# Value products in groups of four key blocks, with the recurrence's tiled products behind them, in a hybrid attention and RWKV-7 encoder block

## Chip, cores and metric

The kernel runs on one core of one Trainium2 chip. The metric is the device time of one execution in microseconds (us). Three runs of the kernel before gave 3750.1, 3751.88 and 3755.33 us; the median is 3751.88 us.

## What is computed

One encoder block over 2048 tokens of width 1024. Two head groups read one input projection: eight heads of softmax attention over two key and value heads, and eight heads of a recurrence (RWKV-7) that runs over the tokens in both directions. Their outputs are joined and projected. Then 16 expert networks each take the 256 tokens that suit them best. The change touches the middle only, where attention and recurrence run beside each other ("the mixers"):

```python
def one_block(qi):                                   # 128 queries
    s = jnp.einsum('bqhgd,bkhd->bhgqk', qi, k) * scale
    p = jax.nn.softmax(s, axis=-1)
    return jnp.einsum('bhgqk,bkhd->bqhgd', p, v)

def step(S, inp):                                    # S: 64 x 64 per head
    r_t, w_t, k_t, v_t, kk_t, a_t = inp
    sa = jnp.einsum('bhvk,bhk->bhv', S, -kk_t)
    S = (S * w_t[:, :, None, :] + sa[..., None] * (kk_t * a_t)[:, :, None, :]
         + v_t[..., None] * k_t[:, :, None, :])
    return S, jnp.einsum('bhvk,bhk->bhv', S, r_t)
```

## The kernel before

The program has four stages: input projection, mixers, output projection, experts. Attention in the mixers goes through 16 blocks, each of two heads and 512 queries (`attention`, `att_out`). One round of `att_out` takes one of 16 key blocks `kb` of 128 keys: scores for both heads into the PSUM tile `st_ps` (lines 694 and 695, two matmuls for each head, since numbers are kept as a high and a low part), one exponential on ScalarE into `pt` (line 696), additions into `acc` for the softmax's sum on VectorE and GpSimd (699), and after every second round the value products of two key blocks into `o_ps` (line 686). A value product has 64 output rows a head, so the two heads take the left and the right half of the array's 128 columns: the profile writes this 128*64, rows times columns of the slice that a matmul uses. `st_ps` has one buffer of two banks, `pt` three.

Beside that, `att_max` finds each query's largest score for the next block (`s_ps`, lines 647 and 648, reduced on VectorE in line 649). The 8 columns of maxima are turned into rows by 8 matmuls with an identity (line 660, 128*2), and ScalarE copies them into rows 64 and 65 of `qa` (662), where the scores' second matmul subtracts them.

The recurrence (`rwkv`) takes 16 sequences of 16 chunks of 64 tokens, four chunks at a time: 64 quarters. `rw_a1` loads `xin`, makes the chunk products of one head after the other (line 846, 64 rows of the array, so 64*128), masks them into `r56` on VectorE (849), transposes `xin` (854) and stores a part for the triangular solve (`rw_solve`, on VectorE or GpSimd). `rq_av` multiplies by 64*64 slices (line 961), `rq_wu` (971), `rq_l` (983) and `rq_step` (999) take the whole array; `rq_step` is the chain from chunk to chunk.

`mixers` calls the two generators in turn, one round of each, four rounds of the recurrence to a quarter, so a quarter lies beside four key blocks. A list scheduler then sets each engine's order: by the order of the calls, unless a block stands under `high_priority`, and by when its own model takes an instruction to be ready. On the chip each engine runs its list in that order. `issue_after(x)`, which the change uses, puts an instruction behind `x` on x's engine.

Of the kernel before, what the change touches and what calls it, by code (L numbers as in the profile page):

```python
# [583 lines left out]
PTB = 3  # L584
# [5 lines left out]
class Attention(Encoder):  # L590
    def attention_pools(self, c):
# [9 lines left out]
        self.kl1 = self.a_k.tile([66, T], F32R, name="kl1")  # L601

# [19 lines left out]
    def att_max(self, j, qc, keys, res):  # L622
# [30 lines left out]
        hl = self.a_q.tile([P, 8, 2], F32R, tag="mhl", name="mhl")  # L653
        nc.vector.tensor_copy(out=hl[:, :, 0], in_=nm)
        nc.vector.tensor_tensor(out=hl[:, :, 1], in0=nm, in1=hl[:, :, 0].bitcast(F32), op=ALU.subtract)
# [19 lines left out]
    def att_out(self, keys, v, q):  # L675
# [7 lines left out]
        def values(kb):  # L683
            pt = pts.pop(kb)
            for h in range(2):
                nc.tensor.matmul(av[64 * h : 64 * h + 64, :], v[:, kb, :], pt[:, h, :], start=(kb == 0), stop=(kb == 15), tile_position=(0, 64 * h))  # L686
# [23 lines left out]
        values(14)  # L710
        values(15)
# [54 lines left out]
class Rwkv(Attention):  # L766
    def rwkv_pools(self, c):
# [4 lines left out]
        slots = {"c": pool("rw_r0", 1)}  # L772
        self.r_m, self.r_x = pool("rw_m"), pool("rw_x", 2)
        slots["a"], slots["b"] = pool("rw_r1", 4), pool("rw_r2", 4)

        of = {(0, 0): "c", (0, 1): "a", (0, 2): "a", (0, 3): "a", (1, 0): "a", (1, 1): "b", (1, 2): "b", (1, 3): "b", (2, 0): "b"}
        for n in range(2, 16):
            for q in range(4):
                if (n, q) not in of:
                    of[n, q] = of[n - 2, q - 1] if q else of[n - 3, 3]  # L780
        self.r56_of = lambda n, q: slots[of[n, q]]
        self.gn_of = slots["b"]
# [43 lines left out]
    def rw_a1(self, n, g):  # L826

        nc = self.nc
        ct, d, half = g["id"]
        c0 = half * GC  # L830
        g["r56"] = {}
        banks = cycle(("pa", "pb", "pc") if n == 1 else ("pa",))
        mask = self.masks[d]
        for i0, q in enumerate(range(4) if d == 0 else range(3, -1, -1)):
            X = self.r_x.tile([P, 2, 512], F32, tag="xin", name="xin")
            r0 = c0 // 2 + 2 * q
            nc.sync.dma_start(out=X, in_=self.d_x[d, ct, :, r0 : r0 + 2, :])
            r56 = self.r56_of(n, i0).tile([P, 4, 384], F32, tag="r56", name="r56")
            g["r56"][q] = r56
            rv = r56.rearrange("p c (x k) -> p c x k", k=64)  # L840
            for h in range(2):
                hs = slice(64 * h, 64 * h + 64)
                p1 = self.bank(next(banks)).tile([P, 4, P], F32, tag="p", name="p1")
                for i in range(4):
                    xr, u = X[hs, i // 2, :], i % 2
                    nc.tensor.matmul(p1[:, i, :].rearrange("p (x k) -> p x k", k=64), xr[:, 128 * u : 128 * u + 128],
                                     xr[:, 256:512].rearrange("p (x u k) -> p x u k", x=2, u=2)[:, :, u, :], start=True, stop=True)
                dst = rv[:, :, 0:3:2, :] if h == 0 else rv[:, :, 3:5, :]
                nc.vector.tensor_tensor(out=dst, in0=p1.rearrange("p c (x k) -> p c x k", k=64),
                                        in1=mask.unsqueeze(1).to_broadcast([P, 4, 2, 64]), op=ALU.mult)  # L850
                yield
            p2 = self.bank(next(banks)).tile([P, 4, P], F32, tag="p", name="p2")
            for i in range(4):
                nc.tensor.transpose(p2[:, i, :], X[:, i // 2, 128 * (i % 2) : 128 * (i % 2) + 128], self.ident)
            nc.scalar.copy(out=rv[:, :, 1:6:4, :], in_=p2.rearrange("p c (x k) -> p c x k", k=64))
            for h in range(2):
                nc.sync.dma_start(out=self.d_a[n, 16 * h + 4 * q : 16 * h + 4 * q + 4].rearrange("c s t -> s c t"), in_=r56[0:64, :, 192 * h : 192 * h + 64])
            yield
# [129 lines left out]
    def rq_step(self, Q, i):  # L988
# [9 lines left out]
        for h in range(2):  # L998
            nc.tensor.matmul(p6[:, c, h, :], lc[:, c, h, :], s0[:, h, :], start=True, stop=True)
# [67 lines left out]
    def rwkv(self):  # L1067
# [23 lines left out]
        for i, (n, k) in enumerate(quarters):  # L1091
# [19 lines left out]
            def extra():  # L1111
                run(a1, 1)
                if k < 3:
# [501 lines left out]
```

## Time and profile before

| | |
|---|---|
| median of three runs | 3751.88 us |
| the profiled execution | 3751.49 us |
| its span, first to last instruction | 3749.8 us |
| TensorE busy | 3509.9 us, 94% |
| VectorE busy | 2516.7 us, 67% |
| ScalarE busy | 1755.2 us, 47% |
| GpSimd busy | 1512.5 us, 40% |
| mean granted TensorE clock | 0.957 of full speed |

Busy is the time in which an engine has at least one instruction under way. TensorE's matmuls overlap, so the time that one adds is read from start to start, not from its own duration; a float32 matmul is recorded as two passes.

### The profile page before, as it was taken

Reading aid. Unit: us, or ns where it says so; the run is one execution under the profiler, and the core shown is the slowest. Engines: PE = TensorE matmul, PEld = TensorE weight load, DVE = VectorE, ACT = ScalarE, POOL = GpSimd, SP = SyncE. Lnnn points to the kernel's source line nnn. Section 1 sums busy time; section 2 is a strip of 40 time slices with the busy share of each in tenths; the row PEclk is TensorE's granted clock in tenths of the full one; section 3 lists DMA queues with packets and bytes.
Section 4 is the critical chain, followed back from the end, with each engine's and each line's share of the span. In section 5 each row is a group of like instructions: output and inputs, shape, how many; then the busy total and the mean of one; then the engine's idle time right before and its main releaser. Section 6 shows DMA issues by size and latency. Waiting matters only on the chain. (4 is left out here: it accounts for less than half of the span.)

```text
span 3749.8 us, 61495 instructions
## 1 busy us (share of the span) xinstructions
PE 3509.9 (94%) x23436; PEld 2856.7 (76%) x23436; DVE 2516.7 (67%) x4289; ACT 1755.2 (47%) x3066; POOL 1512.5 (40%) x1484
## 2 busy tenths in 40 slices
PE   6998899799999999999999997993999999999998
PEld 5887788656666666676666664772999999999997
DVE  6688778876857778558867675447555656655653
ACT  4445444414555555545555564231444444444443
POOL 3445344526263353663364554332332332322321
PEclk8999899879999999999999998996999999999999
DMA  5335334443323433433333232443566766767664
GB/s 182 105 130 168 112 113 141 139 129 73 91 68 79 121 95 85 114 88 87 84 85 85 69 82 82 156 145 113 188 206 205 222 202 216 218 203 222 220 199 127
DMA packets 531228, 510.93 MB, mean 136 GB/s; under 512 B 213304, under 2 KB 449954, under 8 KB 525812
## 3 DMA queue, kind: packets, MB, share of 16 engines
q1 hardware_dynamic: 520612, 472.08, 41.1%
q0 software_dynamic: 10000, 34.91, 4.0%
q8 instruction: 185, 3.03, 0.3%
q14 instruction: 111, 0.91, 0.1%
q10 hardware_dynamic: 320, 0.00, 0.0%
HBM read 392.57 MB, written 109.07 MB: 134 GB/s over the span
## 5 line engine op out<-in xcount | busy, mean ns | idle before, releaser
L1452 DVE TENSOR_TENSOR w_lo<-w_raw,w_hi 128x2048 fp32r<-128x2048 f32 x189 | 432.3, 2293 | 385.8 <-ACT w_hi L1449 385.4
L1516 PE MATMUL gu<-hh,w_lo 128*128 128x256 f32 x2048 | 573.5, 280 | 0.0
L1516 PE MATMUL gu<-hl,w_hi 128*128 128x256 f32 x2048 | 572.7, 280 | 0.0
L1516 PE MATMUL gu<-hh,w_hi 128*128 128x256 f32 x2048 | 572.5, 280 | 0.0
L699 POOL TENSOR_TENSOR acc<-acc,pt 128x512 f32<-128x512 f32 x256 | 354.9, 1391 | 469.0 <-ACT pt L696 456.0
L1449 ACT CAST w_hi<-w_raw 128x2048 fp32r<-128x2048 f32 x192 | 366.9, 1912 | 319.9 <-PE down L1539 133.3
L696 ACT ACTIVATE pt<-st_ps 128x1024 f32<-128x1024 f32 x256 | 262.2, 1024 | 394.8 <-PE st_ps L695 221.2
L649 DVE TENSOR_REDUCE mx<-s_ps 128x1 f32<-128x512 f32 x512 | 342.6, 681 | 149.7 <-PE s_ps L648 148.2
L247 PE MATMUL proj_ps<-hh,w_hi 128*128 128x258 f32 (+1 forms) x1280 | 375.3, 294 | 32.8 <-DVE s_k L265 23.8
L1516 PEld LDWEIGHTS gu<-hh,w_lo 128*128 128x128 f32 x2048 | 388.0, 189 | 0.0
L1516 PEld LDWEIGHTS gu<-hh,w_hi 128*128 128x128 f32 x2048 | 385.6, 188 | 1.3
L1516 PEld LDWEIGHTS gu<-hl,w_hi 128*128 128x128 f32 x2048 | 385.5, 188 | 1.4
L247 PE MATMUL proj_ps<-hl,w_hi 128*128 128x258 f32 (+1 forms) x1280 | 373.0, 292 | 6.4 <-DVE hl L149 5.9
L247 PE MATMUL proj_ps<-hh,w_lo 128*128 128x258 f32 (+1 forms) x1280 | 371.5, 290 | 0.0
L149 POOL TENSOR_TENSOR dl<-hid,dh 128x256 fp32r<-128x256 f32 x128 | 135.1, 1056 | 448.1 <-ACT dh L148 447.8
L686 PE MATMUL o_ps<-pt,av 128*64 128x512 f32 x1024 | 278.5, 627 | 6.7 <-ACT pt L696 6.7
L247 PEld LDWEIGHTS proj_ps<-hh,w_hi 128*128 128x128 f32 x1280 | 250.8, 196 | 41.7 <-issue 23.0
L247 PEld LDWEIGHTS proj_ps<-hl,w_hi 128*128 128x128 f32 x1280 | 251.4, 196 | 10.6 <-DVE hl L149 6.6
L699 DVE TENSOR_TENSOR acc<-acc,pt 128x512 f32<-128x512 f32 x192 | 194.7, 1014 | 91.0 <-ACT pt L696 90.3
L247 PEld LDWEIGHTS proj_ps<-hh,w_lo 128*128 128x128 f32 x1280 | 250.6, 196 | 2.1 <-issue 1.1
L647 PE MATMUL s_ps<-khh,qhl 128*128 128x512 f32 x512 | 240.6, 471 | 9.5 <-DVE mx L649 8.1
L694 PE MATMUL st_ps<-qhl,khh 128*128 128x512 f32 x512 | 229.0, 447 | 2.8 <-ACT pt L696 1.8
(418 smaller groups left out, 8125.1 us busy)
## 6 DMA issues: line engine op xcount, KB each, us to landing
w_raw<-in_w_gate_dram SPq DMA_DIRECT2D x64, 1024.0 KB
w_raw<-in_w_up_e_dram SPq DMA_DIRECT2D x64, 1024.0 KB
w_raw<-in_w_down_dram SPq DMA_DIRECT2D x64, 1024.0 KB
d_x<-X SPq DMA_DIRECT2D x32, 1024.0 KB
xin<-d_x SPq DMA_DIRECT2D x64, 512.0 KB
w_raw<-in_w_in_dram SPq DMA_DIRECT2D x80, 256.0 KB
mod_w<-in_w_ada_dram SPq DMA_DIRECT2D x64, 256.0 KB
mod_w<-in_w_ada_dram SPq DMA_DIRECT2D x8, 1024.0 KB
```

Source lines behind the costliest of these rows:

```text
L149: (eng or nc.gpsimd).tensor_tensor(out=lo, in0=src, in1=hi.bitcast(F32), op=ALU.subtract)
L247: nc.tensor.matmul(acc[:, :n], a[:, kt, :], b[:, kt, lo : lo + n], start=(kt == 0 and m == 0), stop=(kt == KT - 1 and m == 2))
L647: nc.tensor.matmul(s, qs[h][:, ts], khh[:, ks], start=True, stop=False)
L649: nc.vector.tensor_reduce(out=mx[:, 4 * h + qt, kc : kc + 1], in_=s, axis=AX.X, op=ALU.max)
L686: nc.tensor.matmul(av[64 * h : 64 * h + 64, :], v[:, kb, :], pt[:, h, :], start=(kb == 0), stop=(kb == 15), tile_position=(0, 64 * h))
L694: nc.tensor.matmul(s[:, h, :], khh[:, ks], qs[h], start=True, stop=False)
L696: nc.scalar.activation(out=pt, in_=s, func=AF.Exp, scale=0.125)
L699: eng.tensor_tensor(out=acc[:, h, :], in0=(first if kb == 1 else acc)[:, h, :], in1=pt[:, h, :], op=ALU.add)
L1449: nc.scalar.copy(out=hi, in_=raw)
L1452: eng.tensor_tensor(out=lo, in0=raw, in1=hi.bitcast(F32), op=ALU.subtract)
L1516: nc.tensor.matmul(acc[:, m, :], a[:, kt, i * P : (i + 1) * P], b[:, kt, :], start=(kt == 0 and n == 0), stop=(kt == KT - 1 and n == 2))
```

## The change

In `att_out` the value products wait until four key blocks have their exponentials, and then run as one group, the latest block first; `pt` gets a fourth buffer. Behind each group, under the same priority, run the products that the recurrence has put into a list: the 64*64 products of `rq_av` and the 64*128 chunk products, now `a1_products`. Their order changes too: for each chunk head 0 and head 1 alternate, at array rows 0 and 64. They write the two banks of `st_ps`'s buffer instead of a bank of their own. The recurrence's next `rq_step` is put behind them. The chunk work of a sequence is spread over the quarters two sequences ahead, one job a quarter (load, rows, products). The maxima are turned by one transpose (16 rows), written to DRAM and read back into `qa` by two small DMAs. The tile pools of `r56` are arranged anew, and attention skips three turns at the start instead of five.

```diff
-PTB = 3
+PTB = 4
...
-        for h in range(2):
-            pm = self.a_ps.tile([P, 512], F32, tag="s", name="m_ps", bufs=SB)
-            for qt in range(4):
-                nc.tensor.matmul(pm[64:66, qt * P : (qt + 1) * P], hl[:, 4 * h + qt, :].bitcast(F32), self.ident,
-                                 start=True, stop=True, tile_position=(0, 64))
-            nc.scalar.copy(out=q2[h][64:66, :], in_=pm[64:66, :])
-            yield
+        pm = self.a_ps.tile([P, 512], F32, tag="s", name="m_ps", bufs=SB)
+        nc.tensor.transpose(pm[:16, :P], hl.bitcast(F32).rearrange("p h x t -> p (h x t)"), self.ident)
+        mt = self.a_q.tile([16, P], F32, tag="mt", name="mt")
+        nc.scalar.copy(out=mt, in_=pm[:16, :P])
+        nc.sync.dma_start(out=self.d_m[j, qc].rearrange("h x (t p) -> (h x t) p", p=P), in_=mt)
+        yield
+        for h in range(2):
+            nc.sync.dma_start(out=q2[h][64:66, :].bitcast(F32), in_=self.d_m[j, qc, h])
+        yield
...
+        def group(k0):
+            with self.tc.high_priority():
+
+                for kb in (k0 + 3, k0, k0 + 1, k0 + 2):
+                    pt = pts.pop(kb)
+                    for h in range(2):
+                        last = nc.tensor.matmul(av[64 * h : 64 * h + 64, :], v[:, kb, :], pt[:, h, :], start=(kb == 3), stop=(kb == 14), tile_position=(0, 64 * h))
+                with self.tc.issue_after(last.ins):
+                    self.behind = self.flush() or last.ins
...
+            if kb % 4 == 0 and kb:
+                group(kb - 4)
...
-            if kb % 2 == 0 and kb:
-                with self.tc.high_priority():
-                    values(kb - 2)
-                    values(kb - 1)
...
+    def flush(self):
+
+        last = None
+        for job in self.tiled:
+            last = job()
+        self.tiled = []
+        return last
...
+    def a1_products(self, gs, job):
...
+        p1 = self.o_ps.tile([P, 2, 512], F32, tag="st", name="p1", bufs=1)
+        for i in range(4):
             for h in range(2):
...
+                xr, u = X[64 * h : 64 * h + 64, i // 2, :], i % 2
+                last = nc.tensor.matmul(p1[:, h, i * P : (i + 1) * P].rearrange("p (x k) -> p x k", k=64), xr[:, 128 * u : 128 * u + 128],
+                                        xr[:, 256:512].rearrange("p (x u k) -> p x u k", x=2, u=2)[:, :, u, :], start=True, stop=True,
+                                        tile_position=(64 * h, 0))
...
+        self.tiled.append(products)
...
+        with self.tc.issue_after(self.behind) if self.behind else ExitStack():
+            for h in range(2):
+                nc.tensor.matmul(p6[:, c, h, :], lc[:, c, h, :], s0[:, h, :], start=True, stop=True)
+        self.behind = None
...
+            if i + 8 < len(quarters):
+                self.tiled.append(partial(self.a1_products, gs, job))
...
-                if len(streams) == 2 and g is streams[1] and n % 4 == 0 and n <= 20:
+                if len(streams) == 2 and g is streams[1] and n % 4 == 0 and n <= 12:
```

How the order moves on TensorE, in the steady part of the mixers. Before, a piece about a key block long (`av_ps` the 64*64 products, `o_ps` values, `s_ps` with `khh` and `kl1` the maxima, `st_ps` scores, `p1` chunk products of one head, `s_ps2` a step of the recurrence, `wu_ps` the product of `rq_wu`):

```order
L961 MATMUL av_ps_12217<-l56_0_8387,r56_10721 64x64 x8
L686 MATMUL o_ps_12330<-pt_12598,av_8819 64x512 x2
L647 MATMUL s_ps_12558<-khh_8420,qhl_12343 128x512
L648 MATMUL s_ps_12558<-kl1_8312,qa_12345 128x512
L694 MATMUL st_ps_12671<-qhl_11454,khh_8420 128x512
L695 MATMUL st_ps_12671<-qa_11456,kl1_8312 128x512
L694 MATMUL st_ps_12671<-qhl_11463,khh_8420 128x512
L695 MATMUL st_ps_12671<-qa_11465,kl1_8312 128x512
L846 MATMUL p1_12163<-xin_12116 128x128 x4
L999 MATMUL s_ps2_12257<-sr0_8375,lc_12052 128x64 x2
L971 MATMUL wu_ps_12237<-r4_11977,tt1_8370 128x128 x4
L647 MATMUL s_ps_12562<-khh_8420,qhl_12343 128x512
```

The change, around one group (`p1` is now the chunk products of both heads, `p2` the transposes of `xin`; the line numbers are now the changed file's, where 694 is the value product, 648 and 649 the maxima, 865 the chunk product, 988 the 64*64 product):

```order
L694 MATMUL o_ps_12204<-pt_12812,av_8777 64x512 x2
L694 MATMUL o_ps_12204<-pt_12657,av_8777 64x512 x2
L694 MATMUL o_ps_12204<-pt_12708,av_8777 64x512 x2
L694 MATMUL o_ps_12204<-pt_12757,av_8777 64x512 x2
L988 MATMUL av_ps_12845<-l56_1_8386,r56_11461 64x64 x8
L865 MATMUL p1_12891<-xin_12696 128x128 x8
L1030 MATMUL s_ps2_12916<-sr2_8375,lc_12688 128x64 x2
L648 MATMUL s_ps_12728<-khh_8417,qhl_12226 128x512
L649 MATMUL s_ps_12728<-kl1_8312,qa_12228 128x512
L648 MATMUL s_ps_12769<-khh_8417,qhl_12226 128x512
L649 MATMUL s_ps_12769<-kl1_8312,qa_12228 128x512
L852 MATMUL p2_13002<-ident_60,xin_12929 128x128
```

Value products, 64*64 products and chunk products, which stood in three or more places of a quarter, now stand in one run, and whole-array work fills the rest. Over the program, consecutive matmuls that use slices of different size are 1067 before and 490 now.

On VectorE, the masks of those chunk products (`r56<-p1`) now stand in the midst of a solve's steps (`ts`, `ts_t`), straight where the products are due:

```order
L903 TENSOR_TENSOR ts_12509<-ts_12509,ts_t_12795 64x15x16
L901 TENSOR_TENSOR ts_t_12798<-ts_12509 64x238
L903 TENSOR_TENSOR ts_12509<-ts_12509,ts_t_12798 64x14x17
L870 TENSOR_TENSOR r56_12785<-p1_12891,mask1_8359 128x4x2x64
L870 TENSOR_TENSOR r56_12785<-p1_12891,mask1_8359 128x4x128
L901 TENSOR_TENSOR ts_t_12848<-ts_12509 64x234
L650 TENSOR_REDUCE mx_12213<-s_ps_12728 128x1
```

Before, the masks of one head followed its products in a bank that nothing of attention used; now both empty the buffer into which the next scores go.

## Rows read from the trace of the kernel before

**Rows 1.** the page's first part: busy us, share of the span and instructions by engine.

```profile
PE 3509.9 (94%) x23436; PEld 2856.7 (76%) x23436; DVE 2516.7 (67%) x4289; ACT 1755.2 (47%) x3066; POOL 1512.5 (40%) x1484
```

**Rows 2.** windows, one attention block each: length, then busy us (instructions) PE, PEld, DVE, ACT, POOL, PEclk.

```profile
985.10:1079.60 94.50, 92.70 (x561) 63.13 (x560) 57.85 (x77) 51.60 (x104) 56.65 (x76) 0.98 0.34 89
890.20:985.10 94.90, 94.40 (x594) 66.92 (x593) 77.32 (x130) 54.06 (x109) 45.14 (x55) 1.00 0.31 74
1811.30:1909.30 98.00, 96.79 (x551) 65.65 (x550) 80.20 (x150) 51.56 (x103) 36.87 (x28) 0.95 0.34 86
1636.00:1723.00 87.00, 87.00 (x532) 59.99 (x534) 50.88 (x75) 47.51 (x93) 61.62 (x83) 1.00 0.35 84
```

**Rows 3.** timeline of PE at 1062 us: start, us, line, out<-in, slice, shape, passes.

```profile
1062.31 0.40 PE L648 MATMUL s_ps<-kl,qa 66*128 66x512 f32 x1
1062.63 1.08 PE L686 MATMUL o_ps<-pt,av 128*64 128x512 f32 x4
1063.64 0.50 PE L694 MATMUL st_ps<-qhl,khh 128*128 128x512 f32 x1
1063.98 0.40 PE L695 MATMUL st_ps<-qa,kl 66*128 66x512 f32 x1
1064.22 0.40 PE L694 MATMUL st_ps<-qhl,khh 128*128 128x512 f32 x1
...
1065.42 1.16 PE L846 MATMUL p<-xin 64*128 64x128 f32 x8
1066.51 0.50 PE L647 MATMUL s_ps<-khh,qhl 128*128 128x512 f32 x1
1066.85 0.40 PE L648 MATMUL s_ps<-kl,qa 66*128 66x512 f32 x1
...
1067.58 0.68 PE L961 MATMUL av_ps<-l,r 64*64 64x64 f32 x16
1068.19 0.50 PE L694 MATMUL st_ps<-qhl,khh 128*128 128x512 f32 x1
```

**Rows 4.** timeline of PE, products in long runs.

```profile
1301.54 1.97 PE L921 MATMUL x_ps<-rb,z 128*128 128x32 f32 x16 [0.28 <-ACT z L916]
1303.35 0.64 PE L999 MATMUL s_ps<-sr,lc 128*128 128x64 f32 x4
...
1315.66 2.79 PE L686 MATMUL o_ps<-pt,av 128*64 128x512 f32 x12
1318.39 0.50 PE L647 MATMUL s_ps<-khh,qhl 128*128 128x512 f32 x1
```

**Rows 5.** timeline of PE, one block's turning of the maxima and what follows.

```profile
1170.97 1.91 PE L660 MATMUL m_ps<-ident,mhl 128*2 128x128 f32 x16
1172.80 1.16 PE L846 MATMUL p<-xin 64*128 64x128 f32 x8
```

**Rows 6.** groups by line: busy us, mean ns, then idle time before and releasers.

```profile
L846 PE MATMUL p<-xin 64*128 64x128 f32 x1024 | 163.8, 304 | 8.7 <-DVE r L849 4.5 <-DMA xin<-d_x 4.2
...
L849 DVE TENSOR_TENSOR r<-p,mask 128x512 f32<-128x512 f32 x128 | 87.2, 681 | 50.1 <-PE p L846 35.6 <-PE l_ps L983 13.8
```

**Rows 7.** timeline of all engines, the last value products of attention.

```profile
2327.16 0.40 PE L695 MATMUL st_ps<-qa,kl 66*128 66x512 f32 x1
...
2327.66 1.02 ACT L696 ACTIVATE pt<-st_ps 128x1024 f32<-128x1024 f32 x1
...
2328.73 1.08 PE L686 MATMUL o_ps<-pt,av 128*64 128x512 f32 x4 [0.16 <-ACT pt L696]
```

**Rows 8.** timeline of all engines, chunk products and the mask that follows.

```profile
1751.94 0.71 PE L846 MATMUL p<-xin 64*128 64x128 f32 x4
...
1764.88 0.69 DVE L849 TENSOR_TENSOR r<-p,mask 128x512 f32<-128x512 f32 x1
```

**Rows 9.** DMA issues: median us from issue to landing, last.

```profile
d_o<-gn_sq POOLq DMA_DIRECT2D x2, 256.0 KB, 2.7
```

More of the change, by code (lines that the diff above doesn't have):

```diff
@@ L771, in rwkv_pools @@
         pool = lambda name, bufs=1: c.enter_context(tc.tile_pool(name=name, bufs=bufs, reuse_waits="tile"))
-        slots = {"c": pool("rw_r0", 1)}
         self.r_m, self.r_x = pool("rw_m"), pool("rw_x", 2)
[L774 to L782, printed above, removed]
+        self.r56 = [pool("rw_r1", 4), pool("rw_r2", 4)]
         self.a_l = pool("at_l")
@@ L824, in bank @@
         return self.r_ps["abc".index(name[1])]
-    def rw_a1(self, n, g):
-        nc = self.nc
[L829 to L840, printed above, removed]
-            for h in range(2):
[L842 to L857, printed above, removed]
@@ new lines, in flush, with a1_load, a1_rows @@
+    def flush(self):
[4 more added lines that the diff above has]
+        return last
+    def a1_load(self, gs, m):
+        n, i0 = divmod(m, 4)
+        ct, d, half = gs[n]["id"]
+        q = i0 if d == 0 else 3 - i0
+        X = self.r_x.tile([P, 2, 512], F32, tag="xin", name="xin")
+        r0 = half * GC // 2 + 2 * q
+        self.nc.sync.dma_start(out=X, in_=self.d_x[d, ct, :, r0 : r0 + 2, :])
+        return n, i0, q, X
+    def a1_rows(self, gs, job):
+        nc = self.nc
+        n, i0, q, X = job
+        r56 = self.r56[n % 2].tile([P, 4, 384], F32, tag="r56", name="r56")
+        gs[n].setdefault("r56", {})[q] = r56
+        rv = r56.rearrange("p c (x k) -> p c x k", k=64)
+        p2 = self.bank("pa").tile([P, 4, P], F32, tag="p", name="p2")
+        for i in range(4):
+            nc.tensor.transpose(p2[:, i, :], X[:, i // 2, 128 * (i % 2) : 128 * (i % 2) + 128], self.ident)
+        nc.scalar.copy(out=rv[:, :, 1:6:4, :], in_=p2.rearrange("p c (x k) -> p c x k", k=64))
@@ new lines, in a1_products @@
+    def a1_products(self, gs, job):
+        nc = self.nc
+        n, i0, q, X = job
+        r56, mask = gs[n]["r56"][q], self.masks[gs[n]["id"][1]]
+        rv = r56.rearrange("p c (x k) -> p c x k", k=64)
+        p1 = self.o_ps.tile([P, 2, 512], F32, tag="st", name="p1", bufs=1)
+        for i in range(4):
+            for h in range(2):
+                xr, u = X[64 * h : 64 * h + 64, i // 2, :], i % 2
[3 more added lines that the diff above has]
+        for h in range(2):
+            dst = rv[:, :, 0:3:2, :] if h == 0 else rv[:, :, 3:5, :]
+            nc.vector.tensor_tensor(out=dst, in0=p1[:, h, :].rearrange("p (c x k) -> p c x k", x=2, k=64),
+                                    in1=mask.unsqueeze(1).to_broadcast([P, 4, 2, 64]), op=ALU.mult)
+        for h in range(2):
+            nc.sync.dma_start(out=self.d_a[n, 16 * h + 4 * q : 16 * h + 4 * q + 4].rearrange("c s t -> s c t"), in_=r56[0:64, :, 192 * h : 192 * h + 64])
+        return last.ins
@@ L858, in rw_a1 @@
+    def rw_a1(self, gs, jobs):
+        for m in jobs:
+            job = self.a1_load(gs, m)
+            yield
+            self.a1_rows(gs, job)
+            yield
+            self.a1_products(gs, job)
             yield
@@ L997, in rq_step @@
         s1 = self.sr[self.srn % 3]
-        for h in range(2):
-            nc.tensor.matmul(p6[:, c, h, :], lc[:, c, h, :], s0[:, h, :], start=True, stop=True)
+        with self.tc.issue_after(self.behind) if self.behind else ExitStack():
+            for h in range(2):
+                nc.tensor.matmul(p6[:, c, h, :], lc[:, c, h, :], s0[:, h, :], start=True, stop=True)
+        self.behind = None
         for h in range(2):
@@ L1036, in rw_finish @@
             yield
+            if last and nt == 8 and q == 0:
+                yield
+                yield
         nc.vector.tensor_scalar(out=st, in0=st, scalar1=1.0 / 64, scalar2=None, op0=ALU.mult)
@@ L1109, in step, with extra @@
                         self.rq_step(prev, j)
[L1111 to L1113 removed]
+            def extra(j):
+                if k == j == 0:
+                    pass
+                elif k < 3:
                     run(solve, 3)
```

60 lines of the change are left out of this document (33 added, 27 removed).

## Prediction

> **What bounds the kernel now.** First the page's busy shares: TensorE has work under way in 94% of the span, the next engine, VectorE, in 67% [rows 1]. Then the windows of single attention blocks: TensorE is busy 92.70 of 94.50 us, 94.40 of 94.90, 96.79 of 98.00 and all of 87.00, at 0.95 to 1.00 of the clock, while VectorE varies from 50.88 to 80.20 [rows 2]. So in the mixers an instruction that leaves TensorE gives its time back, as long as VectorE keeps up. Busy does not say what a matmul costs, so I read the timeline from start to start.
>
> Where the slice of the array stays the same, a 512-column pass starts 0.24 us after the one before (1063.98 to 1064.22) [rows 3]; a pass on 128 loaded columns takes 1.81 / 16 = 0.113 us even with 32 columns to stream [rows 4], so the load of 128 columns sets its pace. Four value passes take 1.01 us [rows 3], twelve take 2.73 us [rows 4]: eight more cost 1.72, so a pass for each head together costs 0.43 us.
>
> Where the slice changes, time is lost on both sides. Into the value products: 1062.31 to 1062.63 is 0.32 instead of 0.24, then four passes take 1.01 instead of 0.86; out of them, the first score pass takes 0.34 instead of 0.24 [rows 3]. That is 0.33 us for two changes. For chunk products, eight passes take 1.09 instead of 0.90, and the pass after them 0.34 instead of 0.24 [rows 3]. I split this so: **0.09 us** for each change, in which the array empties, and then a weight load that nothing hides, **0.10 us** if the next slice loads 128 columns, **0.05** if it loads 64.
>
> **The change, part by part.**
>
> *Fewer changes of slice.* Counted through both orders, 1067 become 490, 577 fewer, nearly all in the mixers. 577 x 0.09 = 53 us (0.092 unrounded). Of the 577, 369 led to slices that load 128 columns (297 to the whole array, 72 to chunk products): 369 x 0.10 = 37 us. 200 led to 64 columns: 200 x 0.05 = 10 us. The other 8 load next to nothing. Sum: **100 us**.
>
> *Chunk products of two heads in turn.* 1024 passes [rows 6] at 0.113 us one after the other. If head 0 at rows 0 to 63 and head 1 at rows 64 to 127 run at once, 512 pairs remain and 512 x 0.112 = **57 us** go. The trace has no pair of slices in different rows. Pairs in different columns do run at once: 16 passes of line 961 take 0.61 us, changes included [rows 3], where 16 passes on the whole array take 1.81 [rows 4]. Bounds: 0 and 57. I take 57, by the nearest row, line 961, where the loads go together too.
>
> *One transpose of the maxima.* 16 passes take 1.83 us a block [rows 5]; 2 remain. 14 x 0.11 x 16 blocks = **25 us**. ScalarE is spared one of two copies a block, which bounds nothing.
>
> Off TensorE: 100 + 57 + 25 = 182 us. What comes back:
>
> *The group waits for its last exponential.* The last value products began 2328.73 - 2327.16 = 1.57 us after the start of the last score pass, with 1.02 us of ScalarE between [rows 7]; without the pass's own 0.24, some 1.35 to 1.4 us must be filled by other work on TensorE. I priced each order by the rows above and added up what stands there. Between a key block's scores and their value products less than 1.4 us stands in 39 of 256 places (20 before), short by 27 us in sum (13 before): most are the last group of a block, where the search for maxima is over. Between scores and the next scores, which reuse `st_ps`, 48 places (7 before) are short by 16 us (4 before). Added: 43 - 17 = **26 us**.
>
> *Scores wait until the masks have emptied `st_ps`.* Two masks take 2 x 0.681 us on VectorE [rows 6]; with the pipeline's ends 1.7 us at least. Between the chunk products and the next scores the new order holds 2.82 us of work in most of 64 places. Short by 2 us in sum if the masks are done in 1.7 us, 10 at 2.7, 37 at 3.6, 56 at 4.0. VectorE, at 77 to 80 us of a block that will last some 80 instead of 95, will seldom be there at once [rows 2]; but the masks stand under priority. I take **36 us**, for a mean of 3.6, and in it what a fuller VectorE costs elsewhere.
>
> *Maxima through DRAM.* A transfer lands after 2.7 us [rows 9]; two in a row, behind each other in SP's queue, make 5.4 us. In 14 blocks the maxima are done four key blocks early, and this hides; before block 0 and block 8 they are not. Bounds 0 and 11 us; **5 us**, as the recurrence fills part. Behind the waiting read on SP stand loads for a quarter two ahead, the next block's queries and stores for the solve; all are wanted a round or more later.
>
> *At nothing:* loading `xin` half a quarter ahead of its transposes (hidden by the steps between; some 5 us a quarter if not); stores and solve, which begin one round later and have three quarters' time; the fourth `pt` buffer, which is needed for the group and gives nothing else; pools and skipped turns. The output projection and the experts keep their work.
>
> Sum: -182 + 26 + 36 + 5 = -115 us. The profiled execution took 3751.5 us, as good as the median of 3751.88. **Forecast: 3636 us.**
>
> **Rivals.**
> *VectorE keeps up.* The masks are done in time and only the 26 and 5 us come back: 3751.5 - 182 + 31 = 3600 us. For it: VectorE often stood idle before a mask, 35.6 us of waiting for the products [rows 6]. Against it: two of the four blocks above need 77 and 80 us of VectorE [rows 2].
>
> *The two heads' loads follow each other.* Then a pair takes as long as before and 57 us stay: 3636 + 57 = 3693 us. For it: passes are paced by their loads, 0.113 us for 32 streamed columns [rows 4], and 64 rows load no faster than 128 [rows 3, 4]. Against it: line 961. The Trainium skill, "TensorE: Matmul & The Clock Gate", section "LDWEIGHTS (loading the stationary operand)", says that a load's time goes by its columns and not by its rows, which the trace bears out; read as two loads of 128 columns in sequence, it would make the alternation worth nothing.
>
> *The masks hold the scores' buffer, and the kernel gets slower.* Chunk products used a bank of their own, and their mask could be late: one group began at 1751.94 and its mask at 1764.88, 12.9 us on [rows 8]. Now the next scores, and behind them all of TensorE's list, would wait. By the order's work between, a mean of 5.8 us from products to emptied buffer costs 151 us, all that is left (182 - 31); at 7 us it is 222 us, and the time 3751.5 - 151 + 222 = 3822 us. Against it: that mask was late by its place in VectorE's list, which has changed. The Trainium skill, "TensorEngine Tiling (Array Packing)", section "PSUM Bottleneck", warns of this: tiling speeds the products and not the emptying of PSUM. No row here shows it yet.
>
> *Nothing comes of it.* If what TensorE saves turns into waits on VectorE and ScalarE elsewhere, the time stays at 3751 us; the block with 50.88 us of VectorE, which TensorE fills all the same [rows 2], speaks against it.
>
> **How the numbers follow.** Forecast 0.64, VectorE keeps up 0.14, loads in sequence 0.14, slower 0.05, nothing 0.03. The forecast's own range, with the masks at 10 to 56 us and the DRAM path at 0 to 11, is 3605 to 3662. The range takes in the two neighbours: **3590 to 3698 us**. About 0.2% (7.5 us) is what a measurement of this kernel can tell from no change. Faster 0.92, same 0.03, slower 0.05.
>
> **What would show it.** Right: value, 64*64 and chunk products as one run in TensorE's timeline; eight passes a head in about 0.9 us for both heads; blocks of about 84 us; waits of 0.3 to 1.4 us before groups; VectorE near 90% in the heavy blocks. Wrong: pairs of chunk passes 0.22 us apart (loads in sequence); TensorE idle before `st_ps` by several us a group, released by the mask; block times as before with a new releaser.

## The result, and the profile after

The changed kernel takes 3783.53 us (median of 6 runs, 3775.42 to 3788.53); the kernel before took 3753.61 us beside it (6 runs). The ratio is 1.0073, with a 95% interval of 1.0053 to 1.0092: slower by 0.7%, where 3% faster was forecast. The profiled execution took 3788.53 us, 37.0 us more than that of before.

The page's first part, after [rows 1]:

```profile
PE 3415.4 (90%) x23196; PEld 2811.8 (74%) x23196; DVE 2529.6 (67%) x4289; ACT 1737.5 (46%) x3050; POOL 1513.7 (40%) x1484
```

TensorE is busy 94.5 us less and the span is 37 us longer, so it stands still 131 us more. The mean granted clock fell from 0.957 to 0.940. Windows of single attention blocks, with the columns of [rows 2], and as a last row the fifteen blocks from the end of the first to the end of attention:

```profile
905.40:999.70 94.30, 84.77 (x544) 58.96 (x543) 71.73 (x129) 49.74 (x101) 27.55 (x22) 0.96 0.30 70
999.70:1089.30 89.60, 83.08 (x544) 58.49 (x543) 56.92 (x79) 49.86 (x101) 60.48 (x85) 0.96 0.32 83
1849.60:1952.60 103.00, 89.36 (x549) 62.39 (x549) 86.31 (x149) 51.02 (x103) 37.23 (x30) 0.92 0.36 90
905.40:2363.70 1458.30, 1298.68 (x8023) 917.28 (x8023) 1033.87 (x1691) 767.65 (x1552) 692.81 (x765) 0.93 0.34 84
```

The same fifteen blocks of the kernel before:

```profile
890.20:2330.80 1440.60, 1392.34 (x8429) 966.20 (x8428) 1027.47 (x1708) 797.48 (x1601) 714.86 (x800) 0.98 0.35 87
```

Before, TensorE nearly filled a block [rows 2]; now it stands still 9.5, 6.5 and 13.6 us in these three. Length minus busy is 48.3 us before and 159.6 after, **111 us more idle**.

The clock is the second loss. There are two levels, 1.2 and 2.4 GHz. Added up from the single stretches in the two traces, TensorE was at the lower one for 211.6 us of these blocks after and for 68.3 us before, which gives the means of 0.93 and 0.98 above. It was busy in 191.9 and 62.4 us of that; waiting costs nothing more at a low clock. At most half of a busy stretch is lost: 96.0 and 31.2 us, so **65 us more** at most. Score passes at the lower level start 0.43 us apart, where the upper one has 0.24 [rows 3]:

```profile
1103.04 0.63 PE L649 MATMUL s_ps<-kl,qa 66*128 66x512 f32 x1
1103.47 0.63 PE L707 MATMUL st_ps<-qhl,khh 128*128 128x512 f32 x1
```

Did TensorE's work fall as counted? Busy time less what the clock took is 1392.3 - 31.2 = 1361.1 us before and 1298.7 - 96.0 = 1202.7 after: 158 us less, or some more if the clock took less. Counted were 182 for all, 171 for fifteen blocks of sixteen. The timeline of one group, all engines (for before see [rows 3]):

```profile
1115.04 3.65 PE L694 MATMUL o_ps<-pt,av 128*64 128x512 f32 x16
...
1118.62 0.68 PE L988 MATMUL av_ps<-l,r 64*64 64x64 f32 x16
1119.23 1.16 PE L865 MATMUL p<-xin 64*128 64x128 f32 x16
...
1120.32 0.66 PE L1030 MATMUL s_ps<-sr,lc 128*128 128x64 f32 x4
1120.44 1.29 DVE L870 TENSOR_TENSOR r<-p,mask 128x512 f32<-128x512 f32 x2 [4.61 <-PE p L865]
```

Sixteen value passes take 3.58 us, 0.45 for a pass of each head (0.43 was taken). Sixteen chunk passes take 1.09 us, as long as eight took before: slices in different rows do run at once. VectorE stood 4.61 us in front of its masks until the group had come round.

Where TensorE stood still, by what it waited for (the view of waits, 900 to 2330 us: us in total, times, longest), after:

```profile
PE o_ps L694 <- ACT pt L709: 25.7, 17, 2.2
PE st_ps L707 <- DVE r L870: 23.1, 15, 5.6
PE z_ps L940 <- DMA bdr<-d_rt: 22.2, 9, 6.0
PE av_ps L980 <- DVE lc L1016: 18.2, 20, 1.7
PE s_ps L648 <- DVE mx L650: 16.9, 27, 2.6
PE l_ps L1013 <- DVE lc L1016: 13.4, 13, 3.0
PE m_ps L661 <- DVE mhl L657: 4.0, 3, 2.8
...
PE s_ps L1030 <- DVE lc L1016: 3.2, 3, 2.2
```

Rows of the same kinds in that window of the kernel before:

```profile
PE o_ps L686 <- ACT pt L696: 6.1, 9, 1.2
PE p L854 <- DVE r L849: 4.8, 4, 2.2
PE s_ps L999 <- DVE lc L986: 3.5, 6, 1.5
...
PE s_ps L647 <- DVE mx L649: 2.3, 3, 1.1
PE p L846 <- DVE r L849: 2.2, 5, 0.9
PE l_ps L983 <- DVE lc L986: 2.0, 3, 1.0
PE m_ps L660 <- DVE mhl L655: 1.8, 4, 0.7
```

Two of these waits are the group's own (the last exponential; the masks that hold `st_ps`). The others had no terms of their own: the maxima `mx`, `lc` (made from the bank of `rq_l`'s products) and `mhl` (the maxima before they are turned), all from VectorE, and the merge's products, line 940, which join a sequence's solved blocks and wait for a DMA. That last wait shows both losses at once. SyncE's queue, GpSimd and TensorE around it:

```profile
1089.21 2.01 POOL L909 COPY ts_r<-ts 32x1024 f32<-32x1024 f32 x1
...
1093.82 0.43 SPq L912 DMA_DIRECT2D d_rt<-ts_r  x1
...
1096.28 1.34 SPq L873 DMA_DIRECT2D d_a<-r  x2
1097.67 1.59 SPq L925 DMA_DIRECT2D bdr<-d_rt  x3
...
1100.77 0.98 PE L940 MATMUL z_ps<-bdr,bdn 128*128 128x128 f32 x3 [5.98 <-DMA bdr<-d_rt]
```

And the windows of that wait and of what follows:

```profile
1094.80:1100.70 5.90, 0.00 (x0) 0.00 (x0) 0.87 (x2) 1.31 (x4) 0.00 (x0) 0.88 0.74 183
1100.80:1107.40 6.60, 6.60 (x28) 5.83 (x29) 1.83 (x3) 2.27 (x5) 0.83 (x1) 0.60 0.08 22
1107.40:1114.00 6.60, 6.60 (x45) 5.86 (x43) 5.85 (x7) 4.73 (x9) 2.94 (x4) 1.00 0.18 50
```

The solve ends at 1091.2, its last block is stored and read back, and the products start 9.6 us after it, having waited 6 us. Then, for 6.6 us, TensorE is busy at a mean clock of 0.60: 28 instructions, where the next 6.6 us hold 45 (not all of the same kinds). By the clock alone, the wait of 6 us cost at most 0.40 x 6.6 = 2.6 us more.

### The profile page after: what moved, and what is told of

Same layout as the page of the kernel before. It is cut to its first block, busy times and chain, and to the rows that moved or that the text cites. A ratio compares the mean times of both kernels' runs of the same rounds, so it can differ in the third digit from the quotient of the medians.

```text
span 3786.8 us, 61015 instructions
## 1 busy us (share of the span) xinstructions
PE 3415.4 (90%) x23196; PEld 2811.8 (74%) x23196; DVE 2529.6 (67%) x4289; ACT 1737.5 (46%) x3050; POOL 1513.7 (40%) x1484
## 5 line engine op out<-in xcount | busy, mean ns | idle before, releaser
L712 POOL TENSOR_TENSOR acc<-acc,pt 128x512 f32<-128x512 f32 x256 | 346.6, 1359 | 507.2 <-ACT pt L709 471.0
L694 PE MATMUL o_ps<-pt,av 128*64 128x512 f32 x1024 | 269.9, 675 | 27.5 <-ACT pt L709 27.2
```

The lines of the kernel that those rows point to most:

```text
L694: last = nc.tensor.matmul(av[64 * h : 64 * h + 64, :], v[:, kb, :], pt[:, h, :], start=(kb == 3), stop=(kb == 14), tile_position=(0, 64 * h))
L712: eng.tensor_tensor(out=acc[:, h, :], in0=(first if kb == 1 else acc)[:, h, :], in1=pt[:, h, :], op=ALU.add)
```

## The experiments

Three theories. A: the group ties the engines' lists together; VectorE stands before its masks until the group comes, and what stands behind them comes late. B: VectorE has too little time left. C: the masks hold the scores' buffer. A fourth, D, came from the waits above: the solve is late. All ratios are to the kernel before, run beside each, with their intervals.

**Solves on GpSimd**, in the changed kernel (e_pool) and in the one before (b_pool):

```diff
-SOLVE_DVE = (0, 2, 4, 5, 7, 8, 11, 12, 14)
+SOLVE_DVE = (0,)
```

> The changed kernel with every triangular solve but the first on GpSimd: VectorE is spared some 220 us of work in the mixers, GpSimd gets some 270 us more. Theory A (the group ties the engines' lists together: VectorE waits at the masks for the chunk products, and what stands behind the masks comes late): VectorE's share matters little, 3770 to 3790 us, and the stalls of TensorE that VectorE ends (my count: 93 us in the changed kernel) stay over 70 us. Theory B (VectorE has too much to do in a shorter block): those stalls fall under 45 us, the low-clock time with them, 3700 to 3745 us.

> The kernel before with the same move of the solves, as a control. TensorE bounds it and stalls little (58 us by my count), so theories A and B both expect no gain: 3745 to 3775 us; slower by more only if GpSimd, which also adds up the softmax's sums, becomes late.

Measured: 3749.93 us, 0.9982 (0.9966 to 0.9997), 34 us less than the changed kernel; the control 3741.78, 0.9961 (0.9938 to 0.9983), 15 us less than the kernel before beside it. The first lies between the two ranges, the second just under its own: a gain there was foreseen by neither theory. The waits of e_pool, same window:

```profile
PE z_ps L940 <- DMA bdr<-d_rt: 37.5, 9, 6.9
PE o_ps L694 <- ACT pt L709: 28.2, 20, 2.6
PE s_ps L648 <- DVE mx L650: 18.3, 18, 6.1
...
PE st_ps L707 <- DVE r L870: 3.1, 1, 3.1
PE s_ps L1030 <- DVE lc L1016: 3.1, 2, 2.2
PE l_ps L1013 <- DVE lc L1016: 3.0, 5, 1.5
```

Waits for the masks and for `lc` shrink; all that TensorE waits for VectorE falls from 83.5 to 40.9 us. So VectorE's load is a part of it (B), worth some 20 us more here than in the kernel before. It speaks against A that VectorE meanwhile stood longer before its masks, 172.9 us for 134.8 (860 to 2360 us). The maxima don't come sooner, and the wait for the solve grows.

**Chunk products in the maxima's two banks** (e_sbanks), which frees `st_ps` from the masks:

```diff
-        p1 = self.o_ps.tile([P, 2, 512], F32, tag="st", name="p1", bufs=1)
+        p1 = [self.a_ps.tile([P, 512], F32, tag="s", name="p1", bufs=SB) for _ in range(2)]
```

> The changed kernel, but the chunk products write the two banks of the maxima's scores instead of the buffer of the attention's scores. By rows times counts TensorE has 31 us more to do, since the scheduler leaves 657 changes of slice instead of 490. Theory C (the masks hold the buffer of the next scores): the 25 us of stalls before those scores go, with a part of the low clock, and the time falls to 3755 or less in spite of the 31 us. Theories A and B: the wait moves to the maxima's banks, 3790 to 3830 us.

Measured: 3835.68 us, 1.0219 (1.019 to 1.0248). The wait before `st_ps` for the masks is gone, and the maxima, whose banks are shared now, wait 39.2 us instead of 16.9. The row of that wait, and the fifteen blocks:

```profile
PE s_ps L648 <- DVE mx L650: 39.2, 40, 4.1
```

```profile
897.90:2404.00 1506.10, 1390.48 (x8028) 1003.71 (x8028) 1007.81 (x1688) 769.94 (x1557) 700.94 (x762) 0.90 0.33 81
```

Yet waiting is not what made this run slower. TensorE stands still 115.6 us, 44 less than in the changed kernel. Its work, added up as above, is 47 us more, as the order has 657 changes of slice for 490 (some 31 us by the prices of the prediction), and the clock took up to 45 us more with less idle time. So the run does not test C cleanly. What bounds C is the row of the changed kernel: its masks held up TensorE for 23.1 of 159.6 us.

**The tiled products at ordinary priority** (e_prio):

```diff
-                with self.tc.issue_after(last.ins):
-                    self.behind = self.flush() or last.ins
+            with self.tc.issue_after(last.ins):
+                self.behind = self.flush() or last.ins
```

> The changed kernel with the products behind the group (and their masks and copies on VectorE and ScalarE) at ordinary priority instead of high. 551 changes of slice, 10 us more work for TensorE. Theory A: the masks no longer stand early in VectorE's list, its wait for the chunk products falls from 131 us to under 70, and the time falls to 3740 to 3770 us. Theory C: the masks come later and hold the scores' buffer longer, 3800 us or more. Theory B: 3780 to 3800 us.

Measured: 3805.77 us, 1.0127 (1.0107 to 1.0147). Idle in the fifteen blocks is 1471.2 - 1313.0 = 158 us, as in the changed kernel, with 10 us more counted work. The time lies where C put it, but its reason doesn't hold: the wait before `st_ps` for the masks fell to 18.4 us. VectorE's wait before the masks fell from 135 to 99 us, and TensorE gained nothing. Priority isn't the cause.

**Only the masks at ordinary priority** (e_maskord): `a1_products` puts its masks and stores into a second list, which runs after the group's block of priority:

```diff
                 with self.tc.issue_after(last.ins):
                     self.behind = self.flush() or last.ins
+            self.unmask()
...
+        self.masked.append(masks)
```

> The changed kernel with the masks of the chunk products, and the stores behind them, taken out of the group's priority: the group's products keep their place on TensorE, only VectorE's order changes. Theory A (VectorE stands 135 us before these masks, waiting for the group, and the maxima's reductions and the recurrence's lc behind it come late): that wait falls below 90 us, TensorE's waits for mx and lc fall from 63 us to 30 to 45, and the time is 3750 to 3770 us. Rival (the masks then come late, and with them the scores' buffer): TensorE's wait before st_ps for the mask rises from 25 us to 50 or more, and the time is 3790 to 3830 us.

Measured: 3782.19 us, 1.0063 (1.0036 to 1.009). VectorE still stood 139 us before the masks (135 in the changed kernel), so its order hardly changed. Inconclusive on A.

**Chunk products in their own turn** (e_apart):

```diff
-                self.tiled.append(partial(self.a1_products, gs, job))
+                self.a1_products(gs, job)
```

> The changed kernel with the chunk products issued in their own turn and not behind the group; values and 64*64 products stay together. By counted changes of slice TensorE gets 8 us more work. Theory A (it is the tie between the group and the masks that makes VectorE late): VectorE's wait at the masks falls from 135 us below 70, and the time is 3740 to 3770 us in spite of the 8 us. Theory B (VectorE is short of time, wherever the masks stand): 3785 to 3805 us.

Measured: 3798.03 us, 1.0107 (1.0082 to 1.0131). VectorE's wait at the masks fell to 90 us, not below 70, and TensorE gained nothing: 171 us idle in fifteen blocks. The time is in B's range. With e_pool and e_prio, A falls in the form in which it was put: VectorE's idle time before the masks goes up and down without TensorE's waits following it.

**Five solve steps a round** instead of three, alone (e_solve5) and with the solves on GpSimd (e_poolsolve):

```diff
-                    run(solve, 3)
+                    run(solve, 5)
```

> The changed kernel with one number changed: the triangular solve runs five steps a round instead of three, so its last step is issued four rounds earlier and its stores and read-back come earlier too. If the solve that begins one round later is part of the loss (theory D: the nine waits of the merge's products for the transfer of the solved blocks, 23.6 us in the mixers, and the lower granted clock behind each), those waits go and the time falls to 3735 to 3760 us. If that wait only stands in front of another one that ends just as late, or if VectorE, given the steps in a shorter stretch, is the bound (theory B), the time stays at 3775 to 3795 us.

> The changed kernel with all solves but the first on GpSimd and five steps a round. With the solves on GpSimd alone it took 3749.9 us, and there the merge's products still waited 39 us for the transfer of the solved blocks (nine times, up to 7.1 us), the longest item of all. Theory D (those waits are a cost of their own): they go, and the time falls to 3695 to 3720 us. Rival (GpSimd does the solve at its own pace, so issuing it earlier moves nothing, or the next wait ends as late): 3740 to 3755 us.

Measured: 3779.87 us, 1.0056 (1.0033 to 1.0078), and 3759.16 us, 0.9998 (0.9982 to 1.0013). Neither reaches the range of D: the waits stayed (26.9 and 37.4 us before `z_ps`). Read solve by solve in the traces, it isn't the pace that is late but the start. Before, the solve's load went out 5 us ahead of the previous merge's products on the mean and the solve ended 33 us ahead of its own; in the changed kernel the load goes out 24 us after them, and the solve, which takes some 60 us from its load in both, ends 9.5 us ahead (means over 15 merges). The load needs the last chunk products of a sequence, and those now run behind the first group of the next: the last of them ended 10 us ahead of the previous merge's products before and 20 us behind them now (medians), and in most sequences of both kernels the load goes out 3 to 7 us after it. By the code the chunk work can't run further ahead, as the pools of `r56` hold eight tiles where they held nine; a ninth was not tried, so this reason is not shown.

**The merge's products later** (e_latez): behind the quarter's second `rq_l`, the loads where they were.

```diff
+            with self.tc.issue_after(self.behind_l) if n else ExitStack():
+                for i in range(4):
+                    nc.tensor.matmul(pz[:, i, :], bdn[:, 4 * q + i, :], bdr[:, 4 * q + i, :], start=True, stop=True)
...
-                    run(merge, 2)
+                    run(merge, 2 if j else 1)
```

> The changed kernel with the merge's first products put behind the quarter's second lot of rq_l products, some 20 instructions later on TensorE, while the loads of the solved blocks stay where they were. In the changed kernel the solve ends 6.2 to 13.6 us before those products (5.7 to 51 us in the kernel before), and nine of them wait for the load, 23.6 us in all, up to 6.1 us, each followed by a stretch at half clock. Theory D with the clock (a wait costs its length and the slow stretch behind it): the waits fall below 8 us, the time at half clock in the mixers falls by 20 to 50 us, and the time is 3735 to 3760 us. Rival (the solve is what sets the pace, and the next thing that needs it waits as long): 3775 to 3790 us.

Measured: 3759.96 us, 1.0024 (1.0007 to 1.0041), 24 us less than the changed kernel (18 by the ratios). Its waits and its fifteen blocks:

```profile
PE s_ps L648 <- DVE mx L650: 26.2, 38, 2.7
PE l_ps L1014 <- DVE lc L1018: 19.2, 13, 2.7
...
PE z_ps L941 <- DMA bdr<-d_rt: 5.8, 2, 3.8
```

```profile
902.40:2333.30 1430.90, 1283.77 (x8023) 912.23 (x8024) 1021.14 (x1691) 771.05 (x1552) 701.73 (x764) 0.94 0.34 85
```

D holds: the wait went from 22.2 to 5.8 us. A part of it came back before `mx` and `l_ps`, so idle fell by 12.5 us only (147.1), and the clock gave up to 14.

**Three remedies** (e_three): solves on GpSimd, the merge's products later, and the search for maxima spread over a block:

```diff
-                    for _ in range(3):
+                    for _ in range(2 + kb % 2):
```

Control (b_two): the first and the third in the kernel before.

> Three remedies together in the changed kernel: all solves but the first on GpSimd (alone: 3749.9 us), the merge's products later, and the search for maxima spread at 2.5 steps a round instead of 3, so that it fills TensorE nearly to a block's end, where the last group waits for its exponentials (28 us in the run with the solves on GpSimd). If the waits are what gives the saved work back, and each costs a stretch at half clock on top, all three go down and the time is 3690 to 3720 us. If the lost time only moves to the next wait, 3735 to 3755 us.

> Control for the run with three remedies: the kernel before with the two of them that it can take, all solves but the first on GpSimd (alone: 3741.8 us) and the search for maxima spread at 2.5 steps a round. The kernel before has 7 us of waits for the exponentials in the mixers, so the spreading should be worth 0 to 8 us: 3734 to 3745 us. If spreading helps the kernel before as much as it should help the changed one (20 us or more), it is not the group that it mends: below 3725 us.

Measured: 3723.92 us, 0.9928 (0.9904 to 0.9952), and 3731.73 us, 0.9928 (0.9903 to 0.9953). Both beat both kernels, by the same. The fifteen blocks of e_three:

```profile
904.60:2295.40 1390.80, 1261.23 (x8023) 901.91 (x8024) 847.70 (x1195) 767.72 (x1552) 962.21 (x1259) 0.95 0.35 88
```

Idle is 129.6 us at 0.95. The two known remedies gave 34 and 24 us alone; the three give 60, so the spreading adds about nothing here: the groups' waits for the exponential stay at 23.2 us. Neither run is in its range: e_three lies between its two, and b_two, 10 us below b_pool, is 2 us under its own. The blocks of b_two:

```profile
889.80:2313.50 1423.70, 1382.26 (x8429) 961.89 (x8428) 877.59 (x1211) 796.93 (x1602) 983.52 (x1297) 0.98 0.35 88
```

It stands still 41.4 us there. So with the remedies, too, the change still gives back most of the work that it saves.

**One part alone: the transpose of the maxima in the kernel before** (b_maxima), as in the change, with one buffer for `mt`:

```diff
+        nc.tensor.transpose(pm[:16, :P], hl.bitcast(F32).rearrange("p h x t -> p (h x t)"), self.ident)
+        mt = self.a_q.tile([16, P], F32, tag="mt", name="mt", bufs=1)
...
+            nc.sync.dma_start(out=q2[h][64:66, :].bitcast(F32), in_=self.d_m[j, qc, h])
```

> The kernel before with one part of the change alone: the one transpose of the maxima and their way through DRAM. TensorE is spared 23 us by the counted passes. If the saving is paid out where TensorE stays busy: 3728 to 3742 us. If the way through DRAM costs what it saves (the reads wait on SP, and the first block's scores for them): 3748 to 3765 us.

Measured: 3787.34 us, 1.009 (1.0058 to 1.0121), 22 us above the upper of both readings. The opposite, the old turning put back, in the changed kernel (e_oldmax) and on top of the three remedies (e_four):

```diff
+            for qt in range(4):
+                nc.tensor.matmul(pm[64:66, qt * P : (qt + 1) * P], hl[:, 4 * h + qt, :].bitcast(F32), self.ident,
+                                 start=True, stop=True, tile_position=(0, 64))
```

> The changed kernel with the old way of turning the maxima (eight products with the identity a block half, copied straight into the rows), everything else as changed. By counted passes TensorE has 26 us more to do. If the way through DRAM is what made the kernel before slower when it was put there alone (3787 against 3753 us), the time falls by 20 us or more in spite of that: 3740 to 3765 us. If that slowdown came from the order of the list that was drawn anew, and not from the maxima, the 26 us come on top, or are hidden: 3775 to 3815 us.

> The three remedies (solves on GpSimd, the merge's products later, the search for maxima spread out; together 3723.9 us) and the old way of turning the maxima. If the way through DRAM costs more than the passes that it spares, as its part alone suggests: 3690 to 3712 us, the best so far. If the passes count in full: 3740 to 3755 us.

Measured: 3811.59 us, 1.0144 (1.0121 to 1.0167), 28 us above the changed kernel; and 3755.71 us, 1.0004 (0.9985 to 1.0023), 32 us above e_three. So in the change this part is worth about its 26 us of passes or a little more, and the way through DRAM costs next to nothing. The traces agree: in fifteen blocks TensorE's work is 21 and 20 us more with the old turning, and 21 us less in b_maxima. What then slowed b_maxima? Two drawings of the same list at equal work: the kernel before with attention skipping three turns at the start (b_skip12, `n <= 12` as in the change) or six (b_skip24, shown).

```diff
-                if len(streams) == 2 and g is streams[1] and n % 4 == 0 and n <= 20:
+                if len(streams) == 2 and g is streams[1] and n % 4 == 0 and n <= 24:
```

> The kernel before with one number of the change: attention skips three turns at the start instead of five. The counted work of TensorE is the same within 1 us, but 1546 rows of its list differ, about as many as with the maxima's part alone (1449). If a list that is drawn anew costs or gives tens of us by itself: more than 12 us away from 3754. If the order of the list hardly matters at equal work: 3744 to 3764 us, and the 34 us of the maxima's part are its own.

> A second drawing of the same list: the kernel before with attention skipping six turns instead of five, 2 us more counted work on TensorE, 1041 rows of its list different. Same two readings: more than 12 us away from 3754, or 3746 to 3768 us.

Measured: 3753.08 us, 0.9986 (0.9964 to 1.0008), and 3778.89 us, 1.006 (1.0038 to 1.0083). The first stays, the second is 23 us slower with 2 us more counted work. The fifteen blocks of b_skip24 and of b_maxima, in this order:

```profile
889.30:2367.30 1478.00, 1415.12 (x8429) 981.58 (x8429) 1031.19 (x1708) 797.92 (x1601) 723.54 (x800) 0.96 0.34 85
```

```profile
879.30:2352.60 1473.30, 1410.21 (x8233) 973.45 (x8233) 1020.71 (x1706) 783.49 (x1587) 726.42 (x808) 0.95 0.34 84
```

In both, idle rises by 15 us (62.9 and 63.1 for 48.3) and the clock falls to 0.96 and 0.95, which by the stretches at half clock is up to 22 and 39 us more than before. (The execution of b_skip24 that was profiled is its slowest, 8 us above the median.) So an order drawn anew can move this kernel by some 25 us by itself, in waits of a few us and in the clock. That is the likeliest cause for b_maxima, too, but it is not shown: of its waits, those for `lc` grew from 5.5 to 15.0 us, and the part's own reads from DRAM took 3.0. It also bounds what a single run above can say: differences under some 25 us count only where a named row moved with them (the masks and `lc` in e_pool, `z_ps` in e_latez, the maxima's part measured twice). By the same measure the 30 us by which the changed kernel is slower could be those of its drawing; the 152 us that it missed are not.

**The first block**, which ends 15 us later than before (905.4 for 890.2). Its chunk products start at 764.0 us, when the input projection has emptied the banks of `st_ps`, where they started at 724.4. Here the first eight jobs use the recurrence's own two banks (e_start; e_best has the three remedies as well):

```diff
+        if m < 8:
+            p1 = [self.bank(b).tile([P, 512], F32, tag="p", name="p1") for b in ("pb", "pc")]
```

> The changed kernel, with the chunk products of the first two sequences alone in the recurrence's own second and third bank instead of the scores' buffer. In the changed kernel the first chunk product starts at 764.0 us, released by the last emptying of that buffer's banks by the input projection, where it started at 724.4 us before, and the first block ends 15 us later. If that bank is the reason: first chunk product before 735 us, the first block's end at 885 to 898 us instead of 905, and the time 3762 to 3775 us. Rival (the first block waits for the solve or for VectorE as well): its end stays at 900 to 908 us and the time at 3775 to 3790 us. A list drawn anew adds up to 25 us either way to the whole, so the block's end decides, not the total.

> The same remedy on top of the three (solves on GpSimd, the merge's products later, the search for maxima spread out; together 3723.9 us). If the start is a loss of its own: 3700 to 3715 us. If not: 3718 to 3732 us.

Measured: 3779.56 us, 1.0074 (1.0048 to 1.01), and 3729.5 us, 0.9933 (0.991 to 0.9955). Chunk products start at 750.8 us, 13 us sooner but not before 735 as expected, and the block still ends at 903.7: the bank alone isn't the reason. In b_skip12, which has the change's start of attention in the kernel before, the first block ends at 898.2 us, so some 8 of the 15 us may come from that start. The other 7 stay open.

## Why the prediction was wrong

The forecast for the profiled execution was 3636 us, and it took 3788.5: 152 us more.

*What held.* The counted savings of 182 us: some 158 in fifteen blocks where 171 were due. One price was too high: a visit of chunk products is 2 x 0.09 + 2 x 0.10 = 0.38 us by the split, where the rows that it was read from give 0.19 + 0.10 = 0.29; over 72 such changes that is some 6 us. The heads' chunk products do run at once; the rival with the loads in sequence is out. One transpose of the maxima: 20 net of DRAM forecast, 28 and 32 measured. The group's wait for its last exponential: 26 us forecast; 25.7 - 6.1 us before values and some 2 before scores, about 21. The way through DRAM: 5 us forecast, one wait of 3.5 us seen.

*The step that failed.* It is the list "What comes back", in three places.

First, **it had no term for the clock**: every wait was taken at its own length, and every pass at full clock. In the fifteen blocks the clock alone took up to 65 us more. It mostly falls behind waits: of the 35 stretches at half clock that begin between 900 and 2360 us, 30 do so within 5 us of the start of a stop of TensorE of 1 us or more, though only 18% of that time lies so near one (8 of 13 stretches in the kernel before). The Trainium skill, "TensorE: Matmul & The Clock Gate", section "A second HAM failure mode: psum-queue depth-cycling", tells of a kernel in which short stops between groups of matmuls let the clock swing, and says that throughput is lost in going down and up again. The trace agrees: with 111 us more idle time, in short stops, came 23 more stretches at half clock in the fifteen blocks (35 for 12). How much a wait costs this way no run fixes: e_sbanks had 44 us less idle time than the changed kernel and lost up to 45 us more to the clock.

Second, **VectorE elsewhere was undersized**: "36 us, for a mean of 3.6, and in it what a fuller VectorE costs elsewhere". The masks took 23.1 us, inside its bounds. The rest, the waits for `lc`, `mx` and `mhl`, is 18.2 + 16.9 + 13.4 + 4.0 + 3.2 = 55.7 us where 3.5 + 2.3 + 2.0 + 1.8 = 9.6 us stood before: with the masks 69 us for 36, of which 7 us (4.8 + 2.2) had been waits for the masks in their own bank. The block windows on which the prediction rested showed VectorE's busy time, not how soon it answers: VectorE is busy 86.31 of 103.00 us in a heavy block, and TensorE waits for it all the same.

Third, **"stores and solve, which begin one round later and have three quarters' time" stood at nothing**. The slack from the solve's end to the merge was 33 us and became 9.5, as the load starts 29 us later beside the merge before it, and TensorE waited nine times before the merge's products, 22.2 us in all. The time that a step has was looked up in the code; how much of it was left in the trace was not.

The balance, against 152 us: waits 111 where 26 + 36 + 5 = 67 were forecast, 44 us; the clock 65; the first block 26 (15 longer, where its share of the savings, 11, should have made it shorter); behind the last block 4 (3786.8 - 2363.7 against 3749.8 - 2330.8); work in the fifteen blocks, 13 short. Together 152. The sum closes by construction, as the work is what is left of busy time; a smaller loss to the clock would make the work fall by as much more. The 26 us of the first block were not explained beyond the 8 above.

*The rivals.* "Masks hold the scores' buffer" was right in kind and wrong in size: 23 us, not the 222 of that case. The Trainium skill's warning that was cited there, "TensorEngine Tiling (Array Packing)", section "PSUM Bottleneck", is borne out in kind only: emptying the bank of the faster products cost TensorE 23.1 us of waits here. "Nothing comes of it" named the nearest mechanism, waits on VectorE and ScalarE elsewhere, at 0.03: the sign that speaks against it, a block with little VectorE work that TensorE fills, was a fact of an order that the change rewrote. Of the signs announced for being right, one run of products and waits of 0.3 to 1.4 us before groups were seen (up to 2.2); blocks of 84 us became 97.2 on the mean (1458.3 / 15), where 96.0 stood before. Of those for being wrong, block times as before with new releasers is what came.

## What to carry to other kernels

When the bounding engine is full because its order interleaves many short pieces, gathering them saves work on it and takes away the filler between an instruction and the thing that waits for it. Price every wait that this opens, on every queue that feeds the engine, by the slack the trace shows today, and add a term for the clock: here 111 us of new idle time came with up to 65 us lost to it, though e_sbanks shows that the two need not rise together. Where a scheduler draws the order, measure a second drawing at equal work before giving a difference a cause; here it was worth 23 us.

## What the runs showed of the hardware

Products in two row halves of the array run at once even when each must load 128 columns: sixteen passes in 1.09 us, as eight alone.

The clock mostly falls behind short stops: a wait of 6.0 us was followed by 6.6 us at a mean of 0.60, and two other orders of the kernel before with 15 us more idle time in some 1475 us lost up to 22 and 39 us more to the clock. Idle time alone does not set the loss: e_sbanks stood still 115.6 us at a mean of 0.90, the changed kernel 159.6 us at 0.93.
